# A decoder layer's first projection group: block products summed in PSUM instead of a seven-product scheme

## The chip, the cores and the metric

The kernel runs on one core of one Trainium2 chip. The metric is the device time of one execution in microseconds (us). A core has five engines that run their own queues in order: TensorE (PE, with its weight loads PEld), VectorE (DVE), ScalarE (ACT), GpSimd (POOL) and SyncE (SP, which issues most transfers).

## The reference

One decoder layer over 2048 tokens of width 1024. The part that matters here is the first step: RMS norm and one wide input projection.

```python
nx = rmsnorm(h, attn_norm_g[l])
proj = jnp.einsum('bsd,dp->bsp', nx, w_in[l])
gq, gk, gv, gr, glow, dq, dk_, dv_ = jnp.split(proj, split_at, axis=-1)
...
h = h + jnp.einsum('bsm,md->bsd', mixed, w_out[l])
nm = rmsnorm(h, mlp_norm_g[l])
a = jnp.square(jax.nn.relu(jnp.einsum('bsd,df->bsf', nm, w_ff1[l])))
h = h + jnp.einsum('bsf,fd->bsd', a, w_ff2[l])
return rmsnorm(h, final_norm_g)
```

Between the two stand gated linear attention and dilated attention; the change does not touch them.

## The kernel before, in words

**The projection.** The columns of `w_in` are taken in nine groups, each for the first 1024 tokens (tiles 0 to 7 of 128 tokens) and then again for the second 1024. A group is a 2 × 2 block product: tokens 0 to 511 and 512 to 1023, the inner width in two halves of 512, and the columns in two halves of `w` (256, 264 or 128). It is done with seven block products (numbers 1, 2, 5, 6, 3, 4, 7, in this `order`) instead of eight, at the price of sums: sums of weight blocks (in `prep`), sums of token blocks (tiles `TF[j]`/`TB[j]`, made once), and sums of the products (in `product`'s `rest`), for which the four outputs c11, c12, c21, c22 and an accumulator CX lie in SBUF. The list `jobs` numbers the products: 0 to 6 are the first group (`dv`, 256 columns per half), 7 to 13 the second (`gr`, 264), and so on.

**Split operands.** Every operand is split into a high part (ScalarE, a copy that rounds to fp32r) and a remainder (VectorE, a subtraction), and `mm3` does three matmuls per chunk: high·high, low·high, high·low. A block product of one token tile and 256 columns is four chunks, 12 matmuls.

**The first group is written out by hand.** A block of code under `manual_schedule` fixes the order on TensorE, VectorE, ScalarE and GpSimd; SP's order is the planner's. For each token tile: `x_stat` (a Square on ScalarE, a power on GpSimd), `x_scale` (VectorE), `turned` (eight transposes on TensorE into two PSUM banks), `first_half` (splits into the token parts, and for tiles 4 to 7 the differences and sums t1, t2) and `kept` (copies of the raw transposed tile back over `xs`). Token parts 1 and 2 are the two raw halves of the first 512 tokens; 5, 6, 4 and 7 are sums; 3 is the raw lower half of the last 512. Parts 4 and 7 are made late, by `sixth_sum`, `sixth_part` and `last_sums`. Work on ScalarE and VectorE that follows a product (`rest`) is placed by hand too. A weight part is split by `prep(at)`, in one of three rotating tiles `combs`; `load_w` loads a block of raw weights.

**After that the planner orders.** From product 7 on, a loop goes over `jobs`; the engines' order is made by the planner from estimated costs. Beside the products runs `second_half`, which loads, norms, transposes and sums the second 1024 tokens, four pairs of tiles in 24 steps; the list `OTHER` says after which products a step is called. `reload` brings them back near product 56.

Of the kernel before, what the change touches and what calls it, by code (L numbers as in the profile page):

```python
# [11 lines left out]
FR = mybir.dt.float32r  # L12
I32 = mybir.dt.int32
AF = mybir.ActivationFunctionType
OP = mybir.AluOpType
# [3 lines left out]
D = 1024  # L19
# [10 lines left out]
W1AT = 12  # L30
AHEAD, LAG = 3, 2

OTHER = [7, 9, 10, 11, 12, 13] + [14 * k + n for k in (1, 2, 3) for n in (0, 6, 10, 11, 12, 13)]
G0, GE = 8, 56
RELOAD = (10, 11, 12)
BANKS = {"a": 2, "c": 3, "d": 2, "o": 1}
# [2 lines left out]
def emit(tc, a, stop=99):  # L39
# [8 lines left out]
    def ps(tag):  # L48
        return psum.tile([128, 512], F32, name="ps_" + tag, tag=tag, bufs=BANKS[tag])

    def slot(name, dt=F32, n=SLOT):

        return up.tile([128, SLOT], dt, name=name, tag="u", bufs=25)[:, :n]
# [100 lines left out]

    misc = slot("misc")
    gB, gnB, w2b = misc[:, :D], misc[:, D:D + 512], misc[:17, D + 512:D + 768]
    gTs = [misc[:17, D + 768 + 128 * i:D + 896 + 128 * i] for i in range(2)]
# [18 lines left out]
    combs = [slot("wcomb", FR) for _ in range(3)]  # L178
    TF = {j: [slot(f"tb{j}", FR) for _ in range(2 if j < 7 else 1)] for j in order}
    xt = slot("xt")  # L180
    TB = {j: [view(t, (4, 512)) for t in TF[j]] for j in order}
    xs = [t[:, D * q:D * q + D] for t in (xp, bp) for q in range(2)] + [c21[:, :D], last[:, :D]]
    xs += [xt[:, D * q:D * q + D] for q in range(2)]
    nTD = dram.tile([7, 128, 4, 512], F32, name="nTD")

# [8 lines left out]
        t = view(combs[at % 3], (2, 4, max(w, 256)))  # L194
        return [t[:, q, :, :w] for q in range(2)]

    def prep(at, sums=True):

        if at >= len(jobs):
            return  # L200
        g, j = jobs[at]
        kind, _, w = groups[g % NG]
        (a11, a12), (a21, a22) = [[raws[n][:, k, :, :w] for k in range(2)] for n in range(2)]
        hi, lo = comb(at, w)
        src = {1: a11, 2: a12, 5: a21, 6: a21, 3: a12, 4: a22, 7: a21}[j]
        sc = scales.get(kind, 1.0)
        A.activation(hi, src, AF.Copy, scale=sc)  # L207
        if sc == 1.0:
            V.tensor_tensor(lo, src, hi.bitcast(F32), op=OP.subtract)
        else:  # L210
            V.scalar_tensor_tensor(lo, src, sc, hi.bitcast(F32), op0=OP.mult, op1=OP.subtract)
        if j == 2 and g:
            V.tensor_tensor(a21, a21, a22, op=OP.add)
        if j == 5 and sums:
            V.tensor_tensor(a21, a21, a11, op=OP.subtract)
            load_w(g + 1, 0, 0)
            V.tensor_tensor(a12, a12, a21, op=OP.subtract)
        if j == 6:
            V.tensor_tensor(a21, a22, a21, op=OP.subtract)
        if j == 3:  # L220
            load_w(g + 1, 0, 1)
        if j == 4:
            load_w(g + 1, 1, 1)
        if j == 7:
            load_w(g + 1, 1, 0)
# [13 lines left out]

    def outputs(g):  # L240

        return (c11, (c12, c22)[g % 2], c21, (c22, c12)[g % 2])

    def finish(g, n, k, i):
# [36 lines left out]

    banks, held = [0], {}

    def product(at, i):


# [2 lines left out]
        two = w == 256  # L289
        e = i % 2 if two else 0  # L290
        if e == 0:
            held[j, i] = ps("acao"[banks[0] % 4])
            banks[0] += 1
        p = held[j, i - e]
        B, W = TB[j], comb(at, w)
        n = w
# [78 lines left out]

    def x_stat(t):
        ss = stat()
        A.activation(TF[4][0][:, :D], xs[t], AF.Square, accum_out=ss)
        r, X[t] = stat(), stat()
        V.tensor_scalar(r, ss, 1.0 / D, EPS, op0=OP.mult, op1=OP.add)  # L380
        G.tensor_tensor(X[t], r, mhalf, op=OP.pow)
# [24 lines left out]
    def first_half(t, pv):  # L406

        i = t % 4
        b11, b21 = [view(xs[i][:, 512 * q:], (4, 128)) for q in range(2)]
        if t < 4:  # L410
            split(*parts(1, i), pv[0])
            split(*parts(2, i), pv[1])
            return
        t1, t2 = [view(xs[t][:, 512 * q:], (4, 128)) for q in range(2)]
        V.tensor_tensor(t1, pv[0], b11, op=OP.subtract)
        V.tensor_tensor(t2, pv[1], t1, op=OP.subtract)
        split(*parts(5, i), t1)
        split(*parts(6, i), t2)
        split(*parts(3, i), pv[1])

    def sixth_sum(i):
        b21, t2 = [view(xs[k][:, 512:], (4, 128)) for k in (i, i + 4)]
        V.tensor_tensor(b21, b21, t2, op=OP.subtract)

    def sixth_part(i):
        split(*parts(4, i), view(xs[i][:, 512:], (4, 128)))

    def last_sums(i):
        b11, t2 = view(xs[i], (4, 128)), view(xs[i + 4][:, 512:], (4, 128))
# [66 lines left out]
    with tc.manual_schedule(engines={nc.tensor.engine, nc.vector.engine, nc.scalar.engine, nc.gpsimd.engine}):  # L496
        x_load(0, xs[0])
        g1, one = c11[:1, :D], CX[:1, :128]
        A.dma_start(g1, a["attn_norm_g"])
        V.memset(one, 1.0)  # L500
        load_w(0, 0, 0)
        x_load(1, xs[1])
        load_w(0, 0, 1)
        x_load(2, xs[2])
        x_load(3, xs[3])
        load_w(0, 1, 0)
        load_w(0, 1, 1)
        for t in range(4, 8):
            x_load(t, xs[t])
        SP.dma_start(gnB, bcast_row(a["gla_norm_g"], 512))  # L510
        SP.dma_start(w2b[:16], a["gla_gate_w2"].rearrange("o r k -> (o r) k"))
        SP.dma_start(w2b[16:17], a["gla_gate_b"])
        x_stat(0)
        for q in range(2):
            p = ps("a")
            T.matmul(p, one, g1[:, 512 * q:512 * q + 512], start=True, stop=True)
            V.tensor_copy(gB[:, 512 * q:512 * q + 512], p)
        x_scale(0)
        prep(0)

        def turned(t):
            return transposed(xs[t], by=perm)

        x_stat(1)
        pv0 = turned(0)
        split(*parts(1, 0), pv0[0])
        x_scale(1)
        split(*parts(2, 0), pv0[1])
        rest = product(0, 0)
        prep(1)  # L530
        x_stat(2)
        rest()
        pv1 = turned(1)
        kept(0, pv0)
        x_scale(2)
        first_half(1, pv1)
        rest = product(1, 0)
        x_stat(3)
        pv2 = turned(2)
        rest()  # L540
        kept(1, pv1)
        a21, a22 = [raws[1][:, k, :, :256] for k in range(2)]
        V.tensor_tensor(a21, a21, a22, op=OP.add)
        x_scale(3)
        x_stat(4)
        first_half(2, pv2)
        rests = [product(at, 1) for at in (0, 1)]
        pv3 = turned(3)
        for rest in rests:
            rest()  # L550
        kept(2, pv2)
        x_scale(4)
        x_stat(5)
        first_half(3, pv3)
        rests = [product(at, 2) for at in (0, 1)]
        pv4 = turned(4)
        for rest in rests:
            rest()
        kept(3, pv3)
        x_scale(5)  # L560
        prep(2, sums=False)
        x_stat(6)
        first_half(4, pv4)
        for at in (0, 1):
            product(at, 3)()
        pv = turned(5)
        (a11, a12), (a21, a22) = [[raws[n][:, k, :, :256] for k in range(2)] for n in range(2)]
        V.tensor_tensor(a21, a21, a11, op=OP.subtract)
        load_w(1, 0, 0)
        V.tensor_tensor(a12, a12, a21, op=OP.subtract)  # L570
        prep(3)
        prep(4)
        x_stat(7)
        x_scale(6)
        product(2, 0)()
        product(3, 0)()
        first_half(5, pv)
        pv = turned(6)
        product(4, 0)()
        x_scale(7)  # L580
        product(2, 1)()
        first_half(6, pv)
        product(3, 1)()
        pv = turned(7)
        product(4, 1)()
        first_half(7, pv)
        for at in (2, 3, 4):
            product(at, 2)()
        TF[7].append(combs[2])
        TB[7].append(view(TF[7][1], (4, 512)))  # L590
        rests = [product(2, 3)]
        combs[2] = slot("wcomb", FR)
        prep(5)
        sixth_sum(0)
        sixth_sum(1)
        sixth_part(0)
        rests += [product(at, 3) for at in (3, 4)]
        sixth_part(1)
        sixth_sum(2)
        sixth_sum(3)  # L600
        sixth_part(2)
        rests[0]()
        sixth_part(3)
        rests[1]()
        third = rests[2]
        rests = [product(5, i) for i in range(4)]
        prep(6)
        for i in (2, 3, 0):
            last_sums(i)
        for i in range(4):  # L610
            if i == 1:
                last_sums(1)
            if i % 2:
                rests[i]()
            split(*parts(7, i), view(xs[i], (4, 128)))
            if i == 1:
                third()
        rests = [product(6, i) for i in range(4)]
        prep(7)
        for rest in rests:  # L620
            rest()
        prep(8)
    other, back = second_half(), []
    for at in range(7, len(jobs)):
        g = jobs[at][0]
# [2 lines left out]
            back.extend(reload(2 * (at - 7 * NG + 7) + k) for k in range(2))  # L628
        for i in range(4 if groups[g % NG][2] > 128 else 1):
            product(at, i)()  # L630
        if back and at >= 7 * NG - 5:
            back.pop(0)()
            back.pop(0)()
# [896 lines left out]
```

## Time and profile before

| | |
|---|---|
| median of 3 runs | 2313.78 us (2313.0 to 2314.23) |
| profiled execution, its own time | 2312.57 us |
| its span in the profile | 2310.8 us |
| granted TensorE clock, mean | 0.995 |

A row of a group names the line, the engine, the operation, the tiles written and read, the shapes and the count, then busy time and the mean length in ns, then the idle time of the engine before and what ended it. Helpers have one line for all their calls: lines 64 to 66 are `mm3`, 368 and 369 `split`, 393 the transposes, 207 and 209 the split of weights, 325 to 342 what follows a product. Rows of a timeline give start and length; a matmul's length is modelled and overlaps the next one, so the distance of two starts is what counts. In a row of waits, A <- B means that A stood idle until B was done.

### The profile page before, as it was taken

To read this page: it belongs to the slowest core of one execution; us is meant where nothing else is said; L and a number is where in the kernel's file an instruction comes from. 1 tells how busy PE (TensorE), PEld (TensorE's weight loads), DVE (VectorE), ACT (ScalarE), POOL (GpSimd) and SP (SyncE) were. 2 spreads that over 40 slices of the span, in tenths; PEclk is the share of its full clock that TensorE was granted. 3 is DMA by queue.
4 is the path that set the end of the run, shared out by engine and by line. 5 is a ranking of instruction groups with operands and counts; after the bars stand their busy time and mean duration, and the time that the engine had idled before them with its cause. 6 is when DMAs were issued, how large, how long until landed. Compare 5 with 4: busy or idle time off the path is not lost.

```text
span 2310.8 us, 34890 instructions
## 1 busy us (share of the span) xinstructions
PE 2282.6 (99%) x12652; PEld 1975.6 (85%) x12652; DVE 1550.3 (67%) x2863; ACT 1179.3 (51%) x2368; POOL 307.7 (13%) x394
## 2 busy tenths in 40 slices
PE   8999999999999999999999999999999999999998
PEld 7977998799999998888888888888888888888887
DVE  8887778766667676346877788777755346447444
ACT  5574546435877873235555566555543323225224
POOL 1120002025385672000000000000000100000002
PEclk9999999999999999999999999999999999999999
DMA  4457854786668864678644447444486477447553
GB/s 165 144 183 230 250 161 125 215 254 229 209 203 249 253 218 143 210 244 279 208 153 151 151 163 265 151 151 150 150 278 238 155 280 251 148 166 279 188 170 109
DMA packets 341805, 457.59 MB, mean 198 GB/s; under 512 B 18118, under 2 KB 214231, under 8 KB 336257
## 3 DMA queue, kind: packets, MB, share of 16 engines
q1 hardware_dynamic: 336878, 446.71, 59.3%
q10 hardware_dynamic: 4754, 8.66, 1.0%
q8 instruction: 99, 1.62, 0.3%
q14 instruction: 74, 0.60, 0.1%
HBM read 292.99 MB, written 167.02 MB: 199 GB/s over the span
## 4 chain that ended last, share of the span: by engine, by line
PE 51%; ACT 1%; DMA 0%; DVE 0%; issue 0%; DVEq 0%; ACTq 0%
PE ps_c L64 6%; PE ps_c L65 6%; PE ps_c L66 6%; PE ps_a L65 4%; PE ps_a L66 4%; PE ps_d L65 4%; PE ps_d L64 4%; PE ps_a L64 4%; PE ps_d L66 4%; PE ps_o L65 2%; PE ps_o L66 2%; PE ps_o L64 2%; DMA w1raw<-w_ff 0%; ACT scr L1355 0%; DVE hb L369 0%; ACT hb L368 0%
## 5 line engine op out<-in xcount | busy, mean ns | idle before, releaser
L369 DVE TENSOR_TENSOR ca<-ra,ca 128x1024 fp32r<-128x1024 f32 x112 | 138.0, 1233 | 161.6 <-ACT ca L368 161.6
L368 ACT ACTIVATE ca<-ra 128x1024 fp32r<-128x1024 f32 x112 | 118.0, 1053 | 221.3 <-PE ps_c L66 184.3
L368 ACT ACTIVATE w1comb<-w1raw 128x512 fp32r<-128x512 f32 x224 | 140.0, 627 | 153.7 <-PE ps_c L66 55.7
L1357 POOL TENSOR_TENSOR suma<-suma,gs 128x512 f32<-128x512 f32 x16 | 23.4, 1475 | 1393.7 <-ACT scr L1355 1393.7
L369 DVE TENSOR_TENSOR w1comb<-w1raw,w1comb 128x512 fp32r<-128x512 f32 x224 | 153.9, 689 | 51.8 <-ACT w1comb L368 51.7
L785 PE MATMUL ps_a<-v,pt 128*128 128x65 f32 x1200 | 178.2, 252 | 2.5 <-ACT pt L773 1.8
L785 PEld LDWEIGHTS ps_a<-v,pt 128*128 128x128 f32 x1200 | 175.1, 195 | 3.5 <-ACT pt L773 2.1
L757 ACT ACTIVATE pe<-pe,O 128x256 f32<-128x256 f32 (+1 forms) x384 | 156.6, 453 | 39.4 <-DVE O L756 36.1
L766 PE MATMUL ps_d<-ident,pe 128*128 128x128 f32 x600 | 159.9, 279 | 0.0
L756 DVE CUSTOM_DVE_ANT_0 pe<-ps_c,nb 128x256 f32<-128x256 f32 (+1 forms) x384 | 126.9, 361 | 39.6 <-PE ps_d L766 18.4
L207 ACT ACTIVATE wcomb<-wraw 128x512 fp32r<-128x512 f32 (+2 forms) x126 | 97.2, 773 | 88.7 <-PE ps_o L65 22.6
L368 ACT ACTIVATE cb<-rb 128x1024 fp32r<-128x1024 f32 x56 | 59.4, 1060 | 159.3 <-PE ps_o L65 98.8
L66 PE MATMUL ps_c<-cb,ca 128*128 128x512 f32 x336 | 130.7, 389 | 0.0
L66 PE MATMUL ps_c<-hb,w1comb 128*128 128x512 f32 x336 | 130.7, 389 | 0.0
L65 PE MATMUL ps_c<-cb,ca 128*128 128x512 f32 x336 | 130.7, 389 | 0.0
L64 PE MATMUL ps_c<-hb,w1comb 128*128 128x512 f32 x336 | 130.7, 389 | 0.0
L65 PE MATMUL ps_c<-hb,w1comb 128*128 128x512 f32 x336 | 130.7, 389 | 0.0
L64 PE MATMUL ps_c<-cb,ca 128*128 128x512 f32 x336 | 130.7, 389 | 0.0
L766 PEld LDWEIGHTS ps_d<-ident,pe 128*128 128x128 f32 x600 | 110.1, 187 | 0.1
L369 DVE TENSOR_TENSOR cb<-rb,cb 128x1024 fp32r<-128x1024 f32 x56 | 68.3, 1222 | 62.0 <-ACT cb L368 62.0
L1219 ACT ACTIVATE acc<-acc 128x512 f32<-128x512 f32 x128 | 79.6, 631 | 51.5 <-DVE acc L1239 35.8
L64 PE MATMUL ps_a<-wo,mT 128*128 128x512 f32 x256 | 101.3, 396 | 0.0
(419 smaller groups left out, 7038.9 us busy)
## 6 DMA issues: line engine op xcount, KB each, us to landing
ra<-actD SPq DMA_DIRECT2D x56, 1024.0 KB, 6.9
actD<-acc SPq DMA_DIRECT2D x192, 256.0 KB, 2.3
rb<-w_ff SPq DMA_DIRECT2D x72, 512.0 KB, 4.8
w1raw<-w_ff SPq DMA_DIRECT2D x32, 1024.0 KB, 6.2
k<-kD SPq DMA_DIRECT2D x16, 1024.0 KB, 7.9
rb<-hTD SPq DMA_DIRECT2D x13, 1024.0 KB, 7.1
wraw<-w_in SPq DMA_DIRECT2D x48, 256.0 KB, 3.7
cmb<-boD SPq DMA_DIRECT2D x16, 528.0 KB, 7.0
```

Source lines behind the costliest of these rows:

```text
L64: T.matmul(out, sh, mh, start=first, stop=False)
L65: T.matmul(out, sl, mh, start=False, stop=False)
L66: T.matmul(out, sh, ml, start=False, stop=last)
L207: A.activation(hi, src, AF.Copy, scale=sc)
L368: A.activation(hi, src, AF.Copy)
L369: V.tensor_tensor(lo, src, hi.bitcast(F32), op=OP.subtract)
L756: V.tensor_tensor_reduce(p, s, bias, scale=1.0, scalar=BIG, op0=OP.add, op1=OP.min, accum_out=nm)
L757: A.activation(p, p, AF.Exp, bias=nm, scale=-1.0)
L766: T.transpose(pb[:, i * 128:i * 128 + 128], src, ident)
L785: T.matmul(self.b.opsum[:, n % 4], self.pt[:, i * 128:i * 128 + 128], self.b.v[:, blk, cols], start=first, stop=last)
L1219: A.activation(v, v, AF.Relu)
L1357: G.tensor_tensor(C[0], C[0], gF[:, :512], op=OP.mult)
```

## The change

- The first group's seven products become eight plain block products, taken block by block. For each weight half `n` and pair of token tiles one PSUM bank collects both inner halves (`block(n, k, t)`, k = 0 and 1); after the second one ScalarE copies the bank to the output. No weight sums and no output sums are made for this group; its four weight blocks are split once each by `prep_block` into four tiles, one of them the later second tile of part 7.
- Token parts 4 and 3 first hold the two raw halves of tiles 4 to 7 (`first_half`); t1 and t2 are still made there, and their splits into parts 5 and 6 follow in `sum_parts`. Part 4 is filled again with its sum at the end of the first group, and part 7 after products 8 and 9, in the loop.
- The third weight block is loaded ahead of tile 3 of x, and the four loads of the second group's weights are issued together after tile 3's copies.
- The Square in `x_stat` writes to c21, tile 4 of x lies in c22, and CX is an output of the first group.
- `OTHER` calls the 24 steps in four rounds of 11 products, from product 11 to 54, instead of 7 to 55.

```diff
-OTHER = [7, 9, 10, 11, 12, 13] + [14 * k + n for k in (1, 2, 3) for n in (0, 6, 10, 11, 12, 13)]
+OTHER = [11 + 11 * k + n for k in range(4) for n in (0, 5, 7, 8, 9, 10)]
...
+    first_w = [[combs[1], combs[2]], [combs[0], TF[7][1]]]
+    def prep_block(n, k):
+        w = view(first_w[n][k], (2, 4, 256))
+        split(w[:, 0], w[:, 1], raws[n][:, k, :, :256])
+    def block(n, k, t):
+        i, e = t % 4, t % 2
+        if k == e == 0:
+            held["first", n, t] = bank()
+        q = held["first", n, t - e][:, 256 * e:256 * e + 256]
+        B = TB[((1, 2), (4, 3))[t // 4][k]]
+        W = view(first_w[n][k], (2, 4, 256))
+        tk = slice(i * 128, i * 128 + 128)
+        for c in range(4):
+            mm3(q, B[0][:, c, tk], B[1][:, c, tk], W[:, 0, c], W[:, 1, c], k == c == 0, k == 1 and c == 3)
+        if k == e == 1:
+            at = 256 * (i - 1)
+            A.activation(outputs(0)[2 * n + t // 4][:, at:at + 512], held["first", n, t - 1], AF.Copy)
+            for m in (i - 1, i):
+                finish(0, n, t // 4, m)
...
-        split(*parts(5, i), t1)
-        split(*parts(6, i), t2)
-        split(*parts(3, i), pv[1])
+    def sum_parts(i):
+        for q in range(2):
+            split(*parts(5 + q, i), view(xs[i + 4][:, 512 * q:], (4, 128)))
...
+        prep_block(0, 0)
         x_stat(1)
+        pv = turned(0)
+        split(*parts(1, 0), pv[0])
         x_scale(1)
+        split(*parts(2, 0), pv[1])
+        block(0, 0, 0)
+        prep_block(0, 1)
         x_stat(2)
+        prep_block(1, 0)
+        kept(0, pv)
+        pv = turned(1)
+        block(0, 1, 0)
         x_scale(2)
+        first_half(1, pv)
+        block(1, 0, 0)
         x_stat(3)
+        kept(1, pv)
+        pv = turned(2)
+        block(0, 0, 1)
+        block(0, 1, 1)
+        prep_block(1, 1)
         x_scale(3)
+        first_half(2, pv)
+        block(1, 1, 0)
         x_stat(4)
+        kept(2, pv)
+        pv = turned(3)
+        for k in range(2):
+            block(1, k, 1)
...
+        pv = turned(6)
+        for k in range(2):
+            block(0, k, 5)
         x_scale(7)
         first_half(6, pv)
+        sum_parts(2)
         pv = turned(7)
+        for k in range(2):
+            block(0, k, 6)
         first_half(7, pv)
+        for k in range(2):
+            block(0, k, 7)
+        for i in range(4):
             sixth_sum(i)
             last_sums(i)
             if i == 1:
+                prep(7)
+        for k in range(2):
+            block(1, k, 4)
+        sum_parts(3)
         prep(8)
+        for t in (5, 6, 7):
+            for k in range(2):
+                block(1, k, t)
+            split(*parts(4, t - 5), view(xs[t - 5][:, 512:], (4, 128)))
+        split(*parts(4, 3), view(xs[3][:, 512:], (4, 128)))
...
+        if at in (8, 9):
+            for i in range(2 * at - 16, 2 * at - 14):
+                split(*parts(7, i), view(xs[i], (4, 128)))
```

More of the change, by code (lines that the diff above doesn't have):

```diff
@@ L180, in emit @@
     xt = slot("xt")
+    TF[7].append(slot("wcomb", FR))
     TB = {j: [view(t, (4, 512)) for t in TF[j]] for j in order}
-    xs = [t[:, D * q:D * q + D] for t in (xp, bp) for q in range(2)] + [c21[:, :D], last[:, :D]]
+    xs = [t[:, D * q:D * q + D] for t in (xp, bp) for q in range(2)] + [c22[:, :D], last[:, :D]]
     xs += [xt[:, D * q:D * q + D] for q in range(2)]
@@ L195, in comb, with prep @@
         return [t[:, q, :, :w] for q in range(2)]
-    def prep(at, sums=True):
+    def prep(at):
         if at >= len(jobs):
@@ L213, in prep @@
             V.tensor_tensor(a21, a21, a22, op=OP.add)
-        if j == 5 and sums:
+        if j == 5:
             V.tensor_tensor(a21, a21, a11, op=OP.subtract)
@@ L240, in outputs @@
     def outputs(g):
+        if g == 0:
+            return c11, c12, CX, c21
         return (c11, (c12, c22)[g % 2], c21, (c22, c12)[g % 2])
@@ L282, in emit, with bank @@
     banks, held = [0], {}
+    def bank():
+        banks[0] += 1
+        return ps("acao"[banks[0] % 4])
+    first_w = [[combs[1], combs[2]], [combs[0], TF[7][1]]]
[17 more added lines that the diff above has]
+                finish(0, n, t // 4, m)
     def product(at, i):
@@ L291, in product @@
         if e == 0:
-            held[j, i] = ps("acao"[banks[0] % 4])
-            banks[0] += 1
+            held[j, i] = bank()
         p = held[j, i - e]
@@ L377, in x_stat @@
         ss = stat()
-        A.activation(TF[4][0][:, :D], xs[t], AF.Square, accum_out=ss)
+        A.activation(c21[:, :D], xs[t], AF.Square, accum_out=ss)
         r, X[t] = stat(), stat()
@@ L408, in first_half @@
         i = t % 4
-        b11, b21 = [view(xs[i][:, 512 * q:], (4, 128)) for q in range(2)]
         if t < 4:
@@ L414, in first_half @@
         t1, t2 = [view(xs[t][:, 512 * q:], (4, 128)) for q in range(2)]
-        V.tensor_tensor(t1, pv[0], b11, op=OP.subtract)
+        split(*parts(4, i), pv[0])
+        split(*parts(3, i), pv[1])
+        V.tensor_tensor(t1, pv[0], view(xs[i], (4, 128)), op=OP.subtract)
         V.tensor_tensor(t2, pv[1], t1, op=OP.subtract)
-        split(*parts(5, i), t1)
-        split(*parts(6, i), t2)
-        split(*parts(3, i), pv[1])
+    def sum_parts(i):
+        for q in range(2):
+            split(*parts(5 + q, i), view(xs[i + 4][:, 512 * q:], (4, 128)))
     def sixth_sum(i):
@@ L423, in sixth_sum @@
         V.tensor_tensor(b21, b21, t2, op=OP.subtract)
-    def sixth_part(i):
-        split(*parts(4, i), view(xs[i][:, 512:], (4, 128)))
     def last_sums(i):
@@ L504, in emit @@
         x_load(2, xs[2])
+        load_w(0, 1, 0)
         x_load(3, xs[3])
-        load_w(0, 1, 0)
         load_w(0, 1, 1)
@@ L518, in emit @@
         x_scale(0)
-        prep(0)
+        prep_block(0, 0)
         def turned(t):
@@ L524, in emit @@
         x_stat(1)
-        pv0 = turned(0)
-        split(*parts(1, 0), pv0[0])
+        pv = turned(0)
+        split(*parts(1, 0), pv[0])
         x_scale(1)
-        split(*parts(2, 0), pv0[1])
-        rest = product(0, 0)
-        prep(1)
+        split(*parts(2, 0), pv[1])
+        block(0, 0, 0)
+        prep_block(0, 1)
         x_stat(2)
-        rest()
-        pv1 = turned(1)
-        kept(0, pv0)
+        prep_block(1, 0)
+        kept(0, pv)
+        pv = turned(1)
+        block(0, 1, 0)
@@ L535, in emit @@
         x_scale(2)
-        first_half(1, pv1)
-        rest = product(1, 0)
+        first_half(1, pv)
+        block(1, 0, 0)
         x_stat(3)
[L539 to L543, printed above, removed]
+        kept(1, pv)
[3 more added lines that the diff above has]
+        prep_block(1, 1)
         x_scale(3)
+        first_half(2, pv)
+        block(1, 1, 0)
@@ L545, in emit @@
         x_stat(4)
[L546 to L551, printed above, removed]
+        kept(2, pv)
+        pv = turned(3)
+        for k in range(2):
+            block(1, k, 1)
         x_scale(4)
+        first_half(3, pv)
+        for k in range(2):
+            block(0, k, 2)
         x_stat(5)
-        first_half(3, pv3)
-        rests = [product(at, 2) for at in (0, 1)]
-        pv4 = turned(4)
@@ L557, in emit @@
-        for rest in rests:
-            rest()
-        kept(3, pv3)
+        kept(3, pv)
+        for n in range(2):
+            for k in range(2):
+                load_w(1, n, k)
+        pv = turned(4)
+        for k in range(2):
+            block(1, k, 2)
         x_scale(5)
-        prep(2, sums=False)
+        first_half(4, pv)
+        for k in range(2):
+            block(0, k, 3)
         x_stat(6)
-        first_half(4, pv4)
-        for at in (0, 1):
-            product(at, 3)()
+        sum_parts(0)
@@ L566, in emit @@
         pv = turned(5)
[L567 to L572, printed above, removed]
+        for k in range(2):
+            block(1, k, 3)
+        x_scale(6)
+        first_half(5, pv)
+        for k in range(2):
+            block(0, k, 4)
         x_stat(7)
-        x_scale(6)
-        product(2, 0)()
@@ L576, in emit @@
-        product(3, 0)()
-        first_half(5, pv)
+        sum_parts(1)
         pv = turned(6)
-        product(4, 0)()
+        for k in range(2):
+            block(0, k, 5)
         x_scale(7)
-        product(2, 1)()
         first_half(6, pv)
-        product(3, 1)()
+        sum_parts(2)
         pv = turned(7)
-        product(4, 1)()
+        for k in range(2):
+            block(0, k, 6)
         first_half(7, pv)
-        for at in (2, 3, 4):
-            product(at, 2)()
-        TF[7].append(combs[2])
@@ L590, in emit @@
[L590 to L607, printed above, removed]
@@ L608, in emit @@
-        for i in (2, 3, 0):
+        for k in range(2):
+            block(0, k, 7)
+        for i in range(4):
+            sixth_sum(i)
             last_sums(i)
-        for i in range(4):
             if i == 1:
[L612 to L621, printed above, removed]
@@ L622, in emit @@
-        prep(8)
+                prep(7)
+        for k in range(2):
+            block(1, k, 4)
+        sum_parts(3)
+        prep(8)
+        for t in (5, 6, 7):
+            for k in range(2):
+                block(1, k, t)
+            split(*parts(4, t - 5), view(xs[t - 5][:, 512:], (4, 128)))
+        split(*parts(4, 3), view(xs[3][:, 512:], (4, 128)))
     other, back = second_half(), []
```

## The prediction

> **What bounds it now.** I read the page first: its span and its engine shares.
>
> ```profile
> span 2310.8 us, 34890 instructions
> PE 2282.6 (99%) x12652; PEld 1975.6 (85%) x12652; DVE 1550.3 (67%) x2863; ACT 1179.3 (51%) x2368; POOL 307.7 (13%) x394
> ```
>
> TensorE carries the time: it is busy 2282.6 of 2310.8 us, so an engine that is lightened elsewhere gives nothing unless TensorE waits for it. Next the stages by window, cut at the long pauses of the first group, where the change works. Columns: PE, PEld, DVE, ACT, POOL, granted clock, DMA share, GB/s.
>
> ```profile
> 16.54:31.12 14.58, 14.08 (x118) 13.60 (x116) 13.18 (x21) 12.49 (x24) 3.11 (x4) 1.00 0.26 92
> 31.12:33.91 2.79, 0.16 (x2) 0.00 (x0) 2.76 (x3) 1.06 (x1) 0.00 (x0) 1.00 0.29 70
> 33.91:65.05 31.14, 26.40 (x197) 25.73 (x197) 28.24 (x41) 13.11 (x22) 1.52 (x1) 0.89 0.32 92
> 65.05:73.30 8.25, 7.91 (x51) 7.71 (x52) 6.91 (x10) 4.53 (x7) 0.00 (x0) 0.79 0.75 243
> 73.30:2310.80 2237.50, 2222.27 (x12247) 1919.95 (x12246) 1489.02 (x2772) 1137.53 (x2300) 300.26 (x378) 1.00 0.61 199
> ```
>
> From 73.3 us on TensorE idles 15.2 of 2237.5 us at full clock. Before that VectorE is nearly full (28.24 of 31.14 us) while TensorE pauses and its clock falls to 0.89 and 0.79. What it paused for, from the waits of the first 120 us (total, times, longest):
>
> ```profile
> PE ps_c L64 <- ACT wcomb L207: 2.6, 1, 2.6
> PE ps_a L64 <- ACT tb L368: 2.6, 2, 2.4
> PE ps_c L393 <- DVE xt L385: 1.5, 1, 1.5
> ...
> PE ps_c L66 <- DVE wcomb L209: 0.8, 1, 0.8
> PE ps_a L65 <- DVE tb L369: 0.3, 1, 0.3
> PE ps_a L65 <- DVE wcomb L369: 0.3, 1, 0.3
> ```
>
> The first line is the sums of weight blocks, the third a token scaling behind them on VectorE, the 2.4 the sums for the seventh product. Together 8.1 us. Now the prices on TensorE, from its timeline (start, length):
>
> ```profile
> 16.54 0.60 PE L393 MATMUL ps_c<-perm,bp 128*128 128x128 f32 x4
> 16.98 0.60 PE L393 MATMUL ps_d<-perm,bp 128*128 128x128 f32 x4
> 17.33 0.36 PE L64 MATMUL ps_a<-wcomb,tb 128*128 128x256 f32 x1
> ...
> 20.29 0.60 PE L393 MATMUL ps_c<-perm,bp 128*128 128x128 f32 x4
> ...
> 65.05 0.39 PE L64 MATMUL ps_a<-wcomb,tb 128*128 128x256 f32 x1 [2.43 <-ACT tb L368]
> ...
> 66.63 0.41 PE L64 MATMUL ps_a<-wcomb,tb 128*128 128x256 f32 x1
> 67.27 0.41 PE L64 MATMUL ps_a<-wcomb,tb 128*128 128x256 f32 x1
> ...
> 69.77 0.29 PE L64 MATMUL ps_a<-wcomb,tb 128*128 128x256 f32 x1
> 70.14 0.28 PE L64 MATMUL ps_c<-wcomb,tb 128*128 128x256 f32 x1
> 70.49 0.28 PE L64 MATMUL ps_c<-wcomb,tb 128*128 128x256 f32 x1
> ...
> 73.24 0.28 PE L66 MATMUL ps_a<-wcomb,tb 128*128 128x264 f32 x1
> ...
> 116.10 0.39 PE L64 MATMUL ps_a<-tb,wcomb 128*128 128x512 f32 x1
> 116.33 0.40 PE L65 MATMUL ps_a<-tb,wcomb 128*128 128x512 f32 x1
> ```
>
> Three matmuls of one chunk take 0.36 us (70.14 to 70.49), so 12 of them, one product on one token tile, take 1.44. One tile's transposes take 0.79 (16.54 to 17.33); two products after them take 2.96 (17.33 to 20.29), 0.08 more than 2.88. After the 2.43 us pause three take 0.64 (66.63 to 67.27) until 69.77: these 3.1 us hold 14.7 matmuls worth 1.8 us at full pitch, and with its beginning the slow stretch costs about 1.6 us. The second group (264 columns) begins at 73.2; two of its rows stand ahead of that, out of order.
>
> Check of the method on the kernel before: from 16.54 there are 26 products (37.4), six tiles' transposes (4.7) and six times 0.08 (0.5), to 59.1; pauses 8.1; clock lost 11% of 31.14 and 21% of 8.25 (5.2). That is 72.4 against 73.2: the sum misses 0.8.
>
> **The change, part by part.** *More products, fewer sums.* 32 block products of 12 matmuls take the place of 28: 48 more, 4 × 1.44 = 5.8 us, all on TensorE, the bound. VectorE's prices:
>
> ```profile
> L209 DVE TENSOR_TENSOR wcomb<-wraw,wcomb 128x1024 fp32r<-128x1024 f32 x7 | 8.5, 1220 | 0.6 <-ACT wcomb L207 0.4
> ...
> L207 ACT ACTIVATE wcomb<-wraw 128x1024 fp32r<-128x1024 f32 x6 | 6.3, 1052 | 2.4 <-DVE wraw L568 2.1 <-DVE wraw L570 0.3
> ...
> L369 DVE TENSOR_TENSOR tb<-ps_d,tb 128x512 fp32r<-128x512 f32 x8 | 5.5, 683 | 0.0
> ...
> L368 ACT ACTIVATE tb<-ps_d 128x512 fp32r<-128x512 f32 x8 | 4.7, 593 | 0.4 <-PE ps_d L393 0.4
> ```
>
> Gone from VectorE: 14 output sums over 512 columns (0.68 each, 9.5), four weight sums and three weight remainders (1.22 each, 8.5). New: four remainders, since the tiles of the fourth set are filled twice (2.7). Net 15.3 us less, which removes the 8.1 us of pauses. ScalarE copies eight banks instead of six and makes three weight parts fewer: no change that counts, with 18 of 31 us free there.
>
> *The new order on TensorE.* Up to 16.54 it is the old one: tile 0, the first block product, tile 1, the second. Then come 30 block products (43.2), six tiles' transposes (4.7) and 0.5: 64.9 us if nothing waits. Three waits remain.
>
> *Wait 1.* The fourth weight block is split on ScalarE behind the copy of the first finished bank, and that copy waits for TensorE. That ScalarE's queue does stand still for such a copy shows here:
>
> ```profile
> 12.78 0.19 ACT L378 ACTIVATION_READ_ACCUMULATOR tb<-bp 128x1 f32 x1
> ...
> 18.83 0.61 ACT L368 ACTIVATE tb<-ps_c 128x512 fp32r<-128x512 f32 x1
> 19.31 0.61 ACT L368 ACTIVATE tb<-ps_d 128x512 fp32r<-128x512 f32 x1
> ...
> 44.51 0.60 ACT L330 ACTIVATE acc<-ps_a 128x512 f32<-128x512 f32 x1 [3.14 <-PE ps_a L66]
> 45.00 1.14 ACT L368 ACTIVATE tb<-xt 128x512 fp32r<-128x512 f32 x2
> ```
>
> TensorE: 16.54, one product to 17.98, tile 2 to 18.77, two products to 21.73. The copy starts about 21.9 (a matmul's row outlasts its 0.12 pitch by 0.16), frees the queue 0.48 later (18.83 to 19.31), the weight's high part takes 1.05 and the remainder 1.22: 24.7. The next product on TensorE needs both: 3.0 us of pause, behind which tile 3's transposes and everything after stand. It is longer than the 2.43 that was followed by a slow window, so 1.6 more. Bounds: 0 (something lets the split pass the copy) and 6.2 (two slow windows).
>
> *The clock.* The rows say that 2.43 us idle is enough. The Trainium skill, "TensorE: Matmul & The Clock Gate", Part 1, has the clock fall after at least one idle window of about 3.4 us. By that rule the 3.0 us pause would cost no slow window, and the sum would be 1.6 less; the trace disagrees (2.43 us idle, then 0.64 per three), so the rows decide.
>
> *Waits 2 and 3.* Tile 6's splits stand on ScalarE behind the copy that follows the block products on tile 5. After these TensorE has only tile 7's transposes: copy 0.48, high part 0.59, remainder 0.68 and hand-overs 0.2 against 0.79 leave 1.2 us. Then VectorE runs from tile 6's first remainder to tile 7's through six more 512-column operations (0.60 pitch; with its own length some 4.0 in all) against two products (2.9): 1.0 us. Bounds 0 and 4.4, twice my value; I take 2.2, since the prices are of such rows.
>
> *Weights and loads.* The load of the third weight block is issued ahead of tile 3 on SP's queue, in tile 3's old place:
>
> ```profile
> 3.44 1.06 SPq L372 DMA_DIRECT2D bp<-x  x2
> ...
> bp<-x SPq DMA_DIRECT2D x1, 512.0 KB, 8.0
> ```
>
> So it lands by about 12.5, and ScalarE reaches it after the Square of tile 2 (its last row is at 12.78): 0. If it landed at 15, TensorE would wait 0.7 for it at 16.54. Tile 3 slips by one load; its transposes stand behind wait 1, so it may be late by microseconds. The four loads of the next group are issued behind tile 3's copies, before 40 us, and read near 60. The 16 token-row stores are the same number, spread out; SP waits with them, and nothing due soon stands behind.
>
> *Sums moved beside the second group.* The last splits of the fourth and seventh set (2.7 us each on VectorE) run in 66 to 90 us. TensorE needs them five and six products of the second group later, at some 4 × 1.44 = 5.8 us each; the other half's first round leaves this stretch. 0; if that cover were gone, 2.7 each.
>
> *The other half every 11 products.* The same 24 steps; nearly four rounds among the 128-column groups instead of three.
>
> ```profile
> 118.00:250.00 132.00, 131.27 (x605) 103.97 (x604) 108.28 (x184) 76.96 (x161) 13.01 (x8) 1.00 0.68 208
> ```
>
> VectorE is at 0.82. A round is two scalings (1.28) and four sums (0.68), 5.3 us; one more makes 0.86. I take 0; from −0.7 (TensorE's idle in that row) to +6 (below).
>
> **Sum.** 64.9 + 3.0 + 1.6 + 2.2 = 71.7 against 73.2: −1.5; against my own 72.4 for before, −0.7. I take −1.1, between. On the profiled execution (2312.57 us, span 2310.8) that is 2311.5; the median of the runs, 2313.78, lies 1.2 higher: 2312.7 us.
>
> **Rivals.** *No new pause.* If the split of the fourth weight block is not held by the copy, 4.6 us go, and with waits 2 and 3 gone 6.8: 2305.9. For it: VectorE's work falls by 15.3 us and ScalarE only stands waiting there. Against: the row at 44.51, where the queue held its order.
>
> *VectorE becomes the bound in the other half's rounds.* A product over 512 columns takes 12 × 0.233 (116.10 to 116.33) = 2.8. A round now lies within six products (16.8 us) instead of eight, and VectorE, at 0.70 without rounds (three of 5.3 taken off 108.28), needs 0.70 × 16.8 + 5.3 = 17.1 there: 0.3 over, and the transposes follow the scalings after two products (5.6) instead of four, while the Square-to-second-scaling chain took 7.0:
>
> ```profile
> 223.49 1.05 ACT L442 ACTIVATE bp<-xp 128x1024 f32<-128x1024 f32 x1
> ...
> 229.27 1.28 DVE L444 SCALAR_TENSOR_TENSOR xp<-xp,stats,misc 128x1024 f32<-128x1024 f32 x1
> ```
>
> If neither is absorbed, 0.3 + (7.0 − 5.6) = 1.7 per round, 6.8 in all: 2319.5. It decides once TensorE's waits between 118 and 250 us exceed some 6 us. Against: weights are prepared two products ahead.
>
> *The clock stays up over wait 1.* 1.6 less: 2311.1. (The Trainium skill's page on TensorE's clock gate, named above, would have it so.) For it: 16.54 to 31.12 holds 0.5 us of idle time (14.08 of 14.58) at a clock of 1.00. Against: 65.05.
>
> **How the numbers follow.** A change under 0.2%, 4.6 us, is what a measurement of this kernel can hardly tell from none. My forecast has 0.47, the clock rival 0.13 (both within), no new pause 0.24 (faster), rounds on VectorE 0.16 (slower). The likeliest one's own range is 2309 to 2316: one slow window more or less (1.6), waits 2 and 3 gone or doubled (2.2), and a fifth of the 15.2 us of idle time after 73.3, as the planner orders all that anew. Over the cases 2306 to 2318.5, which cuts off the slower case and the edge of the faster one.
>
> **What would show it.** 384 matmuls over 256 columns in the first group; no sums of weight blocks before 60 us; VectorE clearly below full before 60; a TensorE pause of about 3 us near 21.7 released by the weights' split, then a low clock; the 264-column matmuls from about 71.7. Wrong if that pause is missing, if pauses come in every tile, or if TensorE waits on VectorE in the 128-column groups.

## The result, and the profile after

The change made the kernel slower: 2330.68 us (median; 2327.16 to 2332.59) against 2313.39 (2312.56 to 2315.14) for the kernel before on the same chip, a ratio of 1.0073 with a 95% interval of 1.006 to 1.0086. The forecast was 2312.7 (2306.0 to 2318.5), so the time lies 12 us above the range. The profiled execution of after took 2332.59 us; its span is 2330.8.

From the page of after, its span and its engine shares:

```profile
span 2330.8 us, 34977 instructions
...
PE 2288.0 (98%) x12700; PEld 1979.3 (85%) x12700; DVE 1535.9 (66%) x2846; ACT 1181.9 (51%) x2371; POOL 315.0 (14%) x394
```

TensorE has 5.4 us more work and VectorE 14.4 us less, about as forecast (5.8 and 15.3). But TensorE now idles 42.8 us instead of 28.2. To see where, I cut both spans at the same milestones: first transposes, first 264-column matmul, first 512-column matmul (product 14), first 256-column matmul of product 56, first attention matmul, end. Windows of before, with the columns of the prediction's windows:

```profile
8.40:73.20 64.80, 56.44 (x402) 54.41 (x403) 58.56 (x82) 38.05 (x64) 5.72 (x7) 0.92 0.45 148
73.20:116.10 42.90, 42.85 (x354) 42.67 (x352) 37.53 (x60) 27.36 (x67) 7.21 (x8) 1.00 0.50 142
116.10:245.60 129.50, 128.77 (x578) 101.12 (x577) 105.78 (x184) 77.61 (x166) 13.01 (x8) 1.00 0.68 210
245.60:540.60 295.00, 293.58 (x1931) 265.55 (x1930) 215.39 (x348) 135.55 (x252) 39.22 (x39) 1.00 0.65 198
540.60:2310.80 1770.20, 1757.17 (x9392) 1510.70 (x9390) 1130.32 (x2184) 897.01 (x1819) 240.82 (x324) 1.00 0.60 200
```

and of after:

```profile
7.50:70.30 62.80, 59.19 (x451) 57.37 (x452) 44.85 (x65) 37.30 (x66) 5.24 (x7) 0.97 0.49 162
70.30:111.00 40.70, 40.70 (x337) 40.68 (x336) 32.91 (x60) 24.39 (x61) 6.56 (x8) 1.00 0.32 99
111.00:263.00 152.00, 134.19 (x594) 105.53 (x593) 107.64 (x184) 83.39 (x173) 21.93 (x8) 0.94 0.62 192
263.00:561.00 298.00, 295.00 (x1932) 266.98 (x1931) 218.00 (x349) 136.54 (x253) 42.00 (x43) 0.99 0.66 198
561.00:2330.80 1769.80, 1755.19 (x9392) 1507.57 (x9390) 1129.87 (x2184) 896.54 (x1817) 237.55 (x320) 1.00 0.60 200
```

The first group, the one rewritten, is 2.0 us shorter, and VectorE is no longer nearly full in it (44.85 of 62.80). The second group is 2.2 shorter, since a round of the other half's transposes left it. The third stage, whose products the change does not touch, is 22.5 us longer: TensorE idles 17.8 us there instead of 0.7, which is 17.1 of it; the other 5.4 are longer busy time, of which about 2 are that round's transposes, now here, and the rest goes with the granted clock, 0.94 instead of 1.00. The next is 3.0 longer, the rest the same. With the start 0.9 earlier that makes 20.0, the difference of the two spans.

What TensorE waited for, after, in the first 262 us (total, times, longest):

```profile
PE ps_c L424 <- DVE xp L474: 12.0, 1, 12.0
PE ps_a L64 <- ACT acc L361: 2.5, 1, 2.5
...
PE ps_a L64 <- ACT wcomb L399: 1.6, 1, 1.6
...
PE ps_a L64 <- ACT acc L369: 1.4, 1, 1.4
```

The first line is a single wait of the other half's transposes (424) for a token scaling (474). Its chain, backwards. TensorE's timeline of after:

```profile
172.09 0.69 PE L237 MATMUL ps_d<-misc 17*128 17x256 f32 x2
172.71 0.66 PE L424 MATMUL ps_d<-perm,xp 128*128 128x128 f32 x4
174.06 0.66 PE L424 MATMUL ps_d<-perm,xp 128*128 128x128 f32 x4 [0.69 <-ACT bp L478]
186.67 1.12 PE L424 MATMUL ps_c<-perm,xp 128*128 128x128 f32 x4 [11.96 <-DVE xp L474]
```

SP's queue of after, where 488 stores the sums of a round and 403 loads the next round's tokens into the same tile `xp`:

```profile
176.29 2.00 SPq L488 DMA_DIRECT2D nTD<-xp  x3
180.20 1.16 SPq L403 DMA_DIRECT2D xp<-x  x2
```

ScalarE's and VectorE's next rows:

```profile
183.59 1.06 ACT L472 ACTIVATE bp<-xp 128x1024 f32<-128x1024 f32 x1 [8.24 <-DMA xp<-x]
...
185.33 1.28 DVE L474 SCALAR_TENSOR_TENSOR xp<-xp,stats,misc 128x1024 f32<-128x1024 f32 x1 [7.87 <-ACT stats L98]
```

Read upwards: round 2's transposes wait for its scaling, that for the load, that for round 1's stores out of `xp`, and these for round 1's sums. The sums were late because round 1's second half of transposes ran only at 172.71, right behind the gate matmul at 172.09. Both write `ps_d`. The eight `gate` calls that end the second group (lines 230 to 237 of after) take the two "d" banks, and the planner spreads them until 172 us. In before, round 1 was called at products 7 to 13, ahead of all gates; its load for round 2 stands in SP's queue of before at 115:

```profile
109.79 1.44 SPq L458 DMA_DIRECT2D nTD<-xp  x2
...
115.03 0.34 SPq L372 DMA_DIRECT2D xp<-x  x1
```

In after round 1 is called at products 11 to 21 and takes its "d" banks behind the gates: the load comes 65 us later (180.20).

### The profile page after: what moved, and what is told of

Same layout as the page of the kernel before. It is cut to its first block, busy times and chain, and to the rows that moved or that the text cites. A ratio compares the mean times of both kernels' runs of the same rounds, so it can differ in the third digit from the quotient of the medians.

```text
span 2330.8 us, 34977 instructions
## 1 busy us (share of the span) xinstructions
PE 2288.0 (98%) x12700; PEld 1979.3 (85%) x12700; DVE 1535.9 (66%) x2846; ACT 1181.9 (51%) x2371; POOL 315.0 (14%) x394
## 4 chain that ended last, share of the span: by engine, by line
PE 91%; DMA 3%; DVE 3%; ACT 1%; POOL 1%; issue 1%; SPq 0%; DVEq 0%; ACTq 0%; POOLq 0%
PE ps_a L66 10%; PE ps_a L64 10%; PE ps_a L65 10%; PE ps_c L64 8%; PE ps_c L65 8%; PE ps_c L66 8%; PE ps_d L64 4%; PE ps_d L66 4%; PE ps_d L65 4%; PE ps_a L801 4%; PE ps_o L66 4%; PE ps_o L65 4%; PE ps_o L64 4%; PE ps_d L782 2%; PE ps_c L760 2%; PE ps_c L762 2%
## 5 line engine op out<-in xcount | busy, mean ns | idle before, releaser
L209 ACT ACTIVATE wcomb<-wraw 128x512 fp32r<-128x512 f32 (+2 forms) x119 | 90.1, 758 | 101.1 <-PE ps_a L65 38.0
```

## The experiments

Four questions: is it the rounds or the first group; if the rounds, their density or the first one's place; if the place, through which resource; and what is left besides.

**The rounds alone, in the kernel before** (`b_rounds11`).

```diff
-OTHER = [7, 9, 10, 11, 12, 13] + [14 * k + n for k in (1, 2, 3) for n in (0, 6, 10, 11, 12, 13)]
+OTHER = [11 + 11 * k + n for k in range(4) for n in (0, 5, 7, 8, 9, 10)]
```

> The kernel before with nothing changed but the list of the other half's steps (rounds of 11 products from product 11). Theory R (the new rounds cost the time: their first round's second-bank transposes stand behind the eight gates, which hold the two d banks until about 172 us, so that round 2's load, norm and transposes come late): 2325 to 2333 us, with one pause of TensorE of 8 to 14 us near 180 to 190 us released by the scaling of the other half's tiles. Rival F (the first group's new order, or the planner's new order after it, costs the time): 2311 to 2316 us and no such pause.

Measured: 2337.04 us, ratio 1.0103 (1.009 to 1.0117). TensorE's waits:

```profile
PE ps_c L393 <- DVE xp L444: 13.2, 1, 13.2
```

One list costs 24 us with the old first group, 4 us more than theory R allowed, and its long pause is the one of after. The whole loss, and more, comes from the rounds. Beside these rounds the rest of the change gains some 6 us; beside an early first round (`b_pitch11` and `a_first_early` below, both at a ratio of 0.9993) it gains nothing that stands clear of the noise.

**Only the density, in the kernel before** (`b_pitch11`): the first round stays, the others come every 11 products.

```diff
+OTHER = [7, 9, 10, 11, 12, 13] + [11 + 11 * k + n for k in (1, 2, 3) for n in (0, 5, 7, 8, 9, 10)]
```

> The kernel before with its first round where it was (after products 7 to 13, ahead of the gates) and rounds 2 to 4 at 11 products' distance. If only the first round's place behind the gates costs: 2311 to 2317 us. If rounds 2 to 4 at 11 products' distance cost by themselves: 2320 us or more.

Measured: 2312.1 us, 0.9993 (0.9984 to 1.0002). Rounds 2 to 4 at the denser pitch cost nothing here.

**Only the first round's place, in the kernel after** (`a_first_early`).

```diff
+OTHER = [9, 10, 11, 12, 13, 14] + [11 + 11 * k + n for k in (1, 2, 3) for n in (0, 5, 7, 8, 9, 10)]
```

> The changed kernel with only the first round moved ahead of the gates (after products 9 to 14); rounds 2 to 4 stay at 11 products' distance. If the place of the first round behind the gates is what costs (theory R as stated): 2310 to 2316 us. If the denser rounds as such cost (rival D: VectorE over its load in each round, or round 2 itself held by the gates): 2320 us or more.

Measured: 2311.49 us, 0.9993 (0.9984 to 1.0002): some 19 us less than after, by six numbers of the list. Its transposes run at 96 to 105 us, ahead of the first gate.

**The other rounds at the old pitch** (`a_rounds14`).

```diff
+OTHER = [9, 10, 11, 12, 13, 14] + [14 * k + n for k in (1, 2, 3) for n in (1, 6, 10, 11, 12, 13)]
```

> The changed kernel with the rounds of before as far as its late sums let them (first round after products 9 to 14, so its transposes are placed ahead of the gates; then rounds of 14). Theory R: the long pause goes, and what is left is the first group's own gain of 1 to 3 us: 2309 to 2314 us. Rival F: 2326 to 2332 us, as changed.

Measured: 2318.64 us, 1.0025 (1.0016 to 1.0034), between the two expectations. The long pause is gone, but short ones stand in its place:

```profile
PE ps_c L64 <- ACT wcomb L209: 2.9, 1, 2.9
...
PE ps_a L64 <- ACT acc L361: 1.4, 1, 1.4
PE ps_c L424 <- DVE xp L474: 1.3, 1, 1.3
```

The granted clock is 0.95 between 150 and 200 us. So moving round 1 is not the whole of it: against `a_first_early` only the places of rounds 2 to 4 differ, and they cost 7 us. Round 2's first transposes run at 159 and 161 us, while the last gates are still running, but that can't be the reason by itself: in before they run at 157 and 160 us among the same gates, and TensorE waits 0.7 us in all between 116 and 246 us. The reason stays open.

**The bank alone** (`a_c_banks`): the lists of after, but the other half's transposes use the three "c" banks.

```diff
-    def transposed(xt, last=None, pin=False, by=ident):
+    def transposed(xt, last=None, pin=False, by=ident, tags="cd"):
...
-            pv = view(ps("cd"[q]), (4, 128))
+            pv = view(ps(tags[q]), (4, 128))
...
-                for q, pv in enumerate(transposed(xp[:, D * k:], pin=True, by=perm)):
+                for q, pv in enumerate(transposed(xp[:, D * k:], pin=True, by=perm, tags="cc")):
```

> The changed kernel, its rounds as changed, but both transposes of a tile of the other half go to the three c banks, none to the two d banks that the gates use. Theory R (the d banks are the link): round 1's sums no longer wait for the last gate at 172 us, the long pause goes: 2311 to 2317 us. Rival W (VectorE or ScalarE is simply late with the round, whatever the bank): 2325 us or more, sums still near 175 us.

Measured: 2324.43 us, 1.0048 (1.0031 to 1.0064), between the two expectations. The bank is shown to be the link behind the long wait: the 12.0 us are gone and round 2's load is issued at 154.16 instead of 180.20. That gives back some 6 us (the four runs lie between 2317.94 and 2329.05). Some 11 us remain, in short waits:

```profile
PE ps_c L64 <- ACT wcomb L209: 2.4, 1, 2.4
...
PE ps_o L66 <- DVE wcomb L211: 1.6, 1, 1.6
PE ps_a L64 <- ACT acc L361: 1.5, 1, 1.5
```

and in the clock, 0.93 between 150 and 200 us:

```profile
150.00:200.00 50.00, 46.15 (x187) 34.75 (x188) 37.29 (x63) 27.75 (x58) 0.00 (x0) 0.93 0.78 247
```

**GpSimd's product** (`a_c_banks_vmul`). In after a GpSimd product of the second group stretched from 0.72 us to 4.50. Theory P took this for what remained; here VectorE makes that product instead, on top of `a_c_banks`.

```diff
-            G.tensor_tensor(s[:, :m], s[:, :m], gnB[:, j:j + m], op=OP.mult)
+            V.tensor_tensor(s[:, :m], s[:, :m], gnB[:, j:j + m], op=OP.mult)
```

> a_c_banks (2324.4 us) with the gates' neighbour, the product of the gr columns with the norm's weights, on VectorE instead of GpSimd. Theory P (what is left of the loss there is GpSimd's product, stretched from 0.8 to up to 4.5 us while VectorE is full, which holds SP's stores, then ScalarE, then TensorE): 2313 to 2319 us. Rival V (VectorE is simply overloaded from 113 to 150 us; 16 more of its instructions of 0.34 us make that worse): 2325 to 2330 us.

Measured: 2322.99 us, 1.0047 (1.0032 to 1.0061), the same as `a_c_banks`. P fell: the stretched product alone isn't the cost. V, which expected 2325 to 2330 us, isn't borne out either. The 2.4 us wait is gone and one of 2.6 on a gate's copy has come (`ps_d` 237 on VectorE's 235).

**Round 2 later, banks as in after** (`a_round2_late`).

```diff
+OTHER = [11, 16, 18, 19, 20, 21, 26, 31, 34, 35, 36, 37, 38, 42, 44, 45, 46, 47, 48, 51, 52, 53, 54, 55]
```

> The changed kernel, first round as changed (its d transposes still behind the gates, its sums still near 175 us), but rounds 2 to 4 begin four products later, so that round 2's transposes stand at products 34 and 35 instead of 29 and 30 in TensorE's order. Theory R (TensorE meets round 2's transposes before their tiles, which are loaded only when the gates let round 1 finish): the pause of 12.0 us shrinks by some 4 x 2.8 = 11 us, to 0 to 3 us, and the total falls to 2317 to 2324 us, with what the c-bank run also kept. Rival S (the denser later rounds, or a load that stays late by as much): a pause of 6 us or more, 2327 us or more.

Measured: 2329.95 us, 1.0074 (1.0059 to 1.0089). The longest pause fell from 12.0 to 4.7 us, but the total did not move:

```profile
PE ps_c L424 <- DVE xp L474: 7.8, 3, 4.7
PE ps_o L64 <- ACT wcomb L209: 3.5, 1, 3.5
```

Round 1's end slipped as well (its load for round 2 is issued at 188.36 instead of 180.20), and a wait of 3.5 us for a weight split came up. The 2317 to 2324 us of theory R is a miss; the total is the one that rival S named, though the pause is shorter than it said. Giving the late load more products does not recover the time while round 1 itself stands behind the gates.

**Round 1 behind the gates, other banks, four products later** (`a_c_late`, on top of `a_c_banks`): its norm and transposes come at products 20 to 26.

```diff
+OTHER = [11, 20, 23, 24, 25, 26, 27, 31, 33, 34, 35, 36, 37, 41, 43, 44, 45, 46, 47, 50, 52, 53, 54, 55]
```

> a_c_banks (2324.4 us) with the first round's norm and transposes four products later (products 20 to 26 instead of 16 to 21), the later rounds at 10 products' distance. Theory V (what is left of the loss there is that the round's VectorE and ScalarE work meets the second group's finish, 113 to 140 us, when VectorE is full): 2313 to 2319 us. Rival G (the gates themselves, or the later rounds, cost it wherever the first round lies): 2322 us or more.

Measured: 2309.68 us, 0.9985 (0.9976 to 0.9995), 14.8 us under `a_c_banks` and better than expected. The same window as above:

```profile
150.00:200.00 50.00, 48.80 (x228) 39.21 (x227) 42.88 (x68) 30.82 (x62) 0.00 (x0) 1.00 0.82 259
```

This fits theory V, by which the second part of the loss is that round 1's work ran together with the second group's finish, near 115 to 145 us; but the list moved the later rounds too, so it isn't isolated. One way in which it may cost time stands in ScalarE's timeline: copies wait there until stores of older outputs have left the tiles that they write. Before:

```profile
149.77 0.60 ACT L330 ACTIVATE acc<-ps_o 128x512 f32<-128x512 f32 x1 [0.77 <-DMA qD<-acc]
...
157.52 0.60 ACT L338 ACTIVATE acc<-ps_a 128x512 f32<-128x512 f32 x1 [0.77 <-DMA qD<-acc]
```

After:

```profile
154.28 0.60 ACT L361 ACTIVATE acc<-ps_a 128x512 f32<-128x512 f32 x1 [4.77 <-DMA qD<-acc]
...
161.09 0.60 ACT L369 ACTIVATE acc<-ps_c 128x512 f32<-128x512 f32 x1 [1.14 <-DMA qD<-acc]
```

`a_c_banks`:

```profile
149.18 0.63 ACT L260 ACTIVATE acc<-acc 128x512 fp32r<-128x512 f32 x1 [4.51 <-DMA srD<-acc]
...
161.79 0.60 ACT L361 ACTIVATE acc<-ps_a 128x512 f32<-128x512 f32 x1 [3.97 <-DMA qD<-acc]
```

In `a_c_late` ScalarE waits for no such store between 113 and 175 us. No run varied these waits alone, and short ones can be free: in `a_first_early` there are two, of 1.37 and 1.33 us. A full VectorE is not the reason by itself: between 113 and 150 us it was fuller in before (34.51 of 37 us, with TensorE busy for 36.95) than in `a_c_banks` (32.08, with 35.01). GpSimd's stretched product is not it either: in `a_c_banks_vmul`, without it, ScalarE still waits 3.54 and 2.09 us for stores. Which late step held the stores, and how the 14.8 us divide between round 1's place and the other rounds' 10-product pitch, which that list changed too, is open.

**The fourth weight block split earlier** (`a_early_split`, on top of `a_first_early`).

```diff
         pv = turned(2)
+        prep_block(1, 1)
         block(0, 0, 1)
         block(0, 1, 1)
-        prep_block(1, 1)
```

> The changed kernel with the first round ahead of the gates (as in a_first_early, 2311.5 us) and the fourth weight block's split moved ahead of the two block products on tile 1, so that it no longer stands behind the copy of a bank. Theory: the pause of 2.4 us near 22 us goes, and with it the slow clock that sometimes follows (1.6): 2307 to 2310 us. Rival: the pause only moves to the next tile's splits (ScalarE and VectorE are late there instead): 2311 to 2313 us.

Measured: 2308.65 us, 0.9981 (0.9973 to 0.999), the lowest median of all, 0.2% under the kernel before (`a_all` and `a_c_late` lie within the noise of it). TensorE no longer pauses near 22 us, and its first group takes 58.3 us.

**All three together** (`a_all`): `a_early_split` with the "c" banks.

> a_early_split with the other half's transposes in the c banks as well. If the second round, too, waits for the gates' banks in a way that costs: 1 to 3 us below a_early_split. If round 2's wait for the gates is hidden: the same within 2 us.

Measured: 2309.84 us, 0.9985 (0.9976 to 0.9994). The same as `a_early_split`: once round 1 stands ahead of the gates, the bank costs nothing more.

## Why the prediction was wrong, step by step

**The failing step** is "The other half every 11 products", taken as 0 with bounds of −0.7 and +6. Its reasoning was about density: VectorE's share over 118 to 250 us, rounds every 11 products instead of 14. The density of rounds 2 to 4 is in fact free (`b_pitch11`, 0.9993). The list also moved the first round from ahead of the second group's end to behind it, and I counted only that it "leaves this stretch". I did not ask which tiles its transposes shared: the "d" banks with the gates, and `xp` with the next round's load. The rows that would have said so were in the trace of before: round 1's transposes into `ps_d`, the first gate's and the last gate's matmul there, and the transposes of rounds 2 and 3.

```profile
99.44 0.60 PE L393 MATMUL ps_d<-perm,xp 128*128 128x128 f32 x4
...
103.61 0.60 PE L393 MATMUL ps_d<-perm,xp 128*128 128x128 f32 x4
...
115.50 0.27 PE L232 MATMUL ps_d<-ident,acc 128*16 128x128 f32 x1
...
170.29 0.69 PE L235 MATMUL ps_d<-misc 17*128 17x256 f32 x2
170.92 0.66 PE L393 MATMUL ps_d<-perm,xp 128*128 128x128 f32 x4
...
198.05 0.60 PE L393 MATMUL ps_c<-perm,xp 128*128 128x128 f32 x4
```

The last three rows show that a place behind the gates is not enough. In before it is round 2 whose `ps_d` transposes stand right behind the last gate (170.92), and its sums and the next load come late as well:

```profile
182.41 1.30 SPq L372 DMA_DIRECT2D xp<-x  x2
```

That load is 2 us later than the one that held up after (180.20), yet it costs nothing, since TensorE comes to round 3's transposes only at 198.05. In after it stood at round 2's from 174.7 on (186.67 less 11.96). `a_first_early` has its round 2 there too (175.51) and no such pause. So in these runs the long wait came only where both met: a round held by the gates, and the next round's transposes close behind it in TensorE's order. `a_round2_late` agrees, since with these placed four products later the longest pause was 4.7 us; but its total did not fall.

The term measured +24 alone (`b_rounds11`), and 19 for round 1's place in the kernel after (`a_first_early` against after), where 0 stood. Of the 19, some 6 are the bank's (`a_c_banks`). The rest went when round 1 came later and the other rounds at 10 products' distance (`a_c_late`); by which mechanism stays open. The term's upper bound was too low as well: it came from VectorE's surplus, which is not the resource that decided.

**The rival "VectorE becomes the bound in the other half's rounds"** had the sign, and its deciding point (TensorE's waits between 118 and 250 us exceeding some 6 us) was met: 12.0, 2.5 and 1.4 us in the rows above, 15.9. Its mechanism was not: it priced all four rounds alike at 1.7, while one wait of 12.0 in one round carried most, and VectorE itself stood waiting in it (7.87 us before the row at 185.33). TensorE's wait on VectorE in the 128-column groups, which the prediction named as a sign of being wrong, did come, but by this chain.

**The first group came out near its forecast, in part by luck.** From the first transposes to the 264-column products it takes 62.8 us; the forecast's 71.7 less the start of before, 8.4, is 63.3. Two errors offset each other: the idle time was forecast at 5.2 us (3.0 and 2.2) and measured 3.6 (62.80 less 59.19), the busy time at 58.1 (64.9 less 8.4, and 1.6) and measured 59.2. By terms:

- *Products*: 48 more, TensorE +5.4 us for 5.8; VectorE −14.4 for −15.3.
- *Wait 1*: forecast 3.0 us near 21.7 and a slow stretch of 1.6. TensorE's timeline of after:

```profile
22.02 0.39 PE L64 MATMUL ps_a<-wcomb,tb 128*128 128x256 f32 x1 [1.63 <-ACT wcomb L399]
...
23.28 0.58 PE L66 MATMUL ps_a<-wcomb,tb 128*128 128x256 f32 x1 [0.76 <-DVE wcomb L400]
23.66 0.41 PE L64 MATMUL ps_a<-wcomb,tb 128*128 128x256 f32 x1
...
24.30 0.41 PE L64 MATMUL ps_a<-wcomb,tb 128*128 128x256 f32 x1
```

  The cause is as forecast: the weight's split starts on ScalarE at 20.92, behind the bank's copy at 20.43. The pause is 2.4 us, 0.6 less, since TensorE ran the first matmuls while the remainder was made; then three matmuls take 0.64 (23.66 to 24.30) instead of 0.36. Splitting that block earlier takes 2.7 us off the first group against `a_first_early` (61.0 to 58.3) and 4.5 against after; the forecast's two terms were 4.6.
- *Waits 2 and 3*: 2.2 forecast, 1.0 measured (0.23, 0.34 and 0.46 at 51 to 56 us). Oversized, within its bounds.
- *Weights, loads, sums beside the second group*: 0, and no wait for any of them shows.

**The rival "no new pause"** fell for this kernel, but `a_early_split` is its main part made real: with the 4.6 us of wait 1 gone the sum is 2308.1, and 2308.65 was measured. The other 2.2 us, down to 2305.9, did not go: waits 2 and 3 still stand (1.0 us), as in after. That its list of rounds is another makes the closeness partly luck.

**The clock.** I argued from one row that 2.43 us of idle time is enough for a slow window. In after a pause of 2.4 us, in two pieces of 1.63 and 0.76, was followed by one, as its window shows (granted clock 0.93):

```profile
16.54:40.00 23.46, 21.07 (x164) 20.67 (x163) 10.90 (x17) 10.97 (x20) 1.64 (x3) 0.93 0.48 157
```

In `a_first_early` the same pause (1.63 and 0.8 us, 0.3 us earlier) was followed by none:

```profile
16.54:40.00 23.46, 21.07 (x177) 20.65 (x176) 11.14 (x19) 12.73 (x24) 1.98 (x4) 1.00 0.50 161
```

Of the seven kept traces with this pause six have 0.93 in that window and one 1.00. So neither answer was certain, and the term of 1.6 should have been a chance. The Trainium skill, "TensorE: Matmul & The Clock Gate", Part 1, has the activity window run freely, so that the point where the clock rises depends on where in the window the work begins. That the effect of a short pause depends on its place in the same way would fit the two outcomes, but no run here shows it. The same part of the Trainium skill has the clock fall after at least one idle window of about 3.4 us; pauses of 2.4 us that were followed by a slow stretch do not agree with that.

## What to carry to other kernels

When a step is moved in the program, list every buffer it takes (PSUM banks, a tile that the next load overwrites), and see who takes them between the old place and the new: a bank that was free early may be held by an unrelated stream, and the price appears one round later as a late load, if the work that needs this load is met soon after. A share of busy time over a long window says nothing of this; the rows of the first moved instance do. When the costliest part of a change is a list of places, try it alone on the old kernel first: here that one run would have split the change into its gain and its loss.

## What the runs showed of the hardware that was not expected

A GpSimd product over 128x248 took anything from 0.72 to 4.50 us. One row of GpSimd's timeline of before, and then one of after (the profile's spans on GpSimd are rough):

```profile
139.67 0.72 POOL L270 TENSOR_TENSOR acc<-acc,misc 128x248 f32<-128x248 f32 x1 [0.95 <-DVE acc L269]
```

```profile
129.71 4.50 POOL L274 TENSOR_TENSOR acc<-acc,misc 128x248 f32<-128x248 f32 x1 [2.62 <-DVE acc L273]
```

VectorE of after, just behind that start:

```profile
129.90 0.67 DVE L211 TENSOR_TENSOR wcomb<-wraw,wcomb 128x512 fp32r<-128x512 f32 x1
130.50 1.27 DVE L474 SCALAR_TENSOR_TENSOR xp<-xp,stats,misc 128x1024 f32<-128x1024 f32 x1
```

From 129.90 to 133.6 us every VectorE row of after reads only tiles in SBUF, six in a row, and the next one, which reads PSUM, starts at 133.55, 0.7 us before GpSimd's row ends. VectorE was nearly as busy beside the 0.72 us of before, but with a MEMSET, a copy out of PSUM and an instruction with one input in PSUM. Between 113 and 150 us GpSimd's eight products took 20.94 us in after and 11.49 in `a_c_late`. The Trainium skill, "SBUF — State Buffer", "Who interferes with whom", says that a VectorE instruction with two SBUF inputs and a GpSimd instruction that reads SBUF shut each other out through a shared port. The stretch fits that, as VectorE's row here with `wraw` and `wcomb`, both in SBUF, is one of several within those 4.50 us. No run here isolated it, and taking the product off GpSimd did not change the time.
